# A streaming contrast adjustment: twelve tiles of 32 KB rows become eight tiles of 48 KB rows

## The chip, the cores and the metric

The kernel runs on one core of a Trainium2 chip. The metric is device time in microseconds (us), the median of several runs. A profiled execution gives one more time, together with its span: the time from the first to the last instruction on the core.

The engines that matter are DVE (VectorE), ACT (ScalarE), PE (TensorE), POOL (GpSimd) and the queue of SP (SyncE). Here SP issues all loads and ACT issues all stores. Sixteen DMA engines move the data of both.

## The reference

```python
x: (16, 3, 512, 512) float32, factor = 1.5
mean = np.mean(x, axis=(2, 3), keepdims=True)
return np.clip(mean + factor * (x - mean), 0, 1).astype(np.float32)
```

There are 48 images (16 x 3) of 262,144 pixels. Each image needs its own mean before the first of its pixels can be written. For one image the result is `clip(factor * x + shift, 0, 1)` with `shift = (1 - factor) * mean`. The input and the output have 50.33 MB each.

## The kernel before

The whole input is taken as a flat array. A tile is 128 partitions x 8192 floats: 32 KB in each partition, 4 MB in all. An image then fills 32 partitions, a tile holds four images, and there are twelve tiles. One tensor `ring` in SBUF has six slots of one tile each (192 KB in a partition); tile t uses slot t % 6, and everything is done in place.

For each tile:

- `load` (L82) copies a tile into its slot, issued on SP. At the start six tiles are asked for in four transfers: tiles 0 and 1 alone, then 2 with 3, and 4 with 5. A later load waits until the store that last used its slot has landed.
- `add` (L87 to L100) makes one sum for each partition. ACT copies the slot onto itself and accumulates (L96). PE multiplies these sums by `blockw`, a 128 x 128 matrix that is `(1 - factor) / pixels` inside each 32 x 32 block and zero elsewhere, so that column t of the PSUM tile `bias` holds in every partition the shift of its image (L100). For tile 0 DVE sums the first 4352 columns (L91) beside ACT, and two matmuls are accumulated.
- `clip` (L102 to L114) is two DVE instructions: multiply by the factor and add the shift, which is read from PSUM (L104), then clamp to 0 and 1 (L112).
- `store` (L85) writes the slot back, issued on ACT.

The order on each engine is that of the program text. Tile 0 is clipped and stored in three pieces, of 1024, 2048 and 5120 columns (rows of 4, 8 and 20 KB). Then comes the loop over tiles, L126 to L135: clip of tile t, `add` of tile t+1, store of tile t, load of tile t+5; for t = 1 and 3 the store stands ahead of the `add`. Since the store and the ACT part of `add` are on one queue, a store that stands behind `add(t + 1)` is issued only after tile t+1 has landed and been summed.

Of the kernel before, what the change touches and what calls it, by code (L numbers as in the profile page):

```python
# [1 line left out]

# [4 lines left out]


P = 128  # L10
ROW = 8192
BUFS = 6
FIRST = (1024, 3072)


@with_exitstack
def kernel(
    ctx: ExitStack,
    tc: tile.TileContext,
    x: bass.AP,  # L20
    factor: float,
    out: bass.AP,
):

    nc = tc.nc
    f32 = mybir.dt.float32
    Alu = mybir.AluOpType
    Act = mybir.ActivationFunctionType  # L30

    B, C, H, W = x.shape
    n_img, n_pix = B * C, H * W
    ppi = n_pix // ROW
    per_tile = P // ppi
    n_tiles = n_img // per_tile
    assert ppi * ROW == n_pix and per_tile * n_tiles == n_img

    factor = float(factor)
    wconst = (1.0 - factor) / float(n_pix)  # L40

    x_f = x.rearrange("b c h w -> (b c h w)")
    out_f = out.rearrange("b c h w -> (b c h w)")

    def dram(ap, t, c0=0, c1=ROW, n=1):
        run = [[P * ROW, n]] if n > 1 else []
        return bass.AP(
            tensor=ap.tensor, offset=t * P * ROW + c0, ap=[[ROW, P], *run, [1, c1 - c0]]
        )

    consts = ctx.enter_context(tc.tile_pool(name="consts", bufs=1))
    xpool = ctx.enter_context(tc.tile_pool(name="xpool", bufs=1))
    small = ctx.enter_context(tc.tile_pool(name="small", bufs=1))
    psum = ctx.enter_context(tc.tile_pool(name="psum", bufs=1, space=bass.MemoryType.PSUM))


    sums = small.tile([P, 2 * n_tiles], f32, name="sums")
    bias = psum.tile([P, n_tiles], f32, name="bias")

    blockw = consts.tile([P, P], f32, name="blockw")  # L60
    blocks = blockw.rearrange("p (a b) -> p a b", b=ppi)
    nc.gpsimd.memset(blockw, wconst)  # L62
    for base, step in ((0, -ppi), (ppi - 1, ppi)):
        nc.gpsimd.affine_select(  # L64
            out=blocks,
            in_=blocks,
            compare_op=Alu.is_ge,
            fill=0.0,
            base=base,
            pattern=[[step, per_tile], [0, ppi]],  # L70
            channel_multiplier=1 if step < 0 else -1,
        )


    ring = xpool.tile([P, BUFS, ROW], f32, name="ring")

    def slots(t, n=1, c0=0, c1=ROW):
        k = t % BUFS
        return ring[:, k, c0:c1] if n == 1 else ring[:, k : k + n, :]

    def load(t, n=1):
        nc.sync.dma_start(out=slots(t, n), in_=dram(x_f, t, n=n))  # L82

    def store(t, c0=0, c1=ROW):
        nc.scalar.dma_start(out=dram(out_f, t, c0, c1), in_=slots(t, 1, c0, c1))  # L85

    def add(t, c0=0):  # L87
        own = sums[:, 2 * t : 2 * t + 2]
        parts = []
        if c0:  # L90
            nc.vector.tensor_reduce(  # L91
                out=own[:, 0:1], in_=slots(t, 1, 0, c0), axis=mybir.AxisListType.X, op=Alu.add
            )
            parts.append(own[:, 0:1])
        part = slots(t, 1, c0)
        nc.scalar.activation(out=part, in_=part, func=Act.Copy, accum_out=own[:, 1:2])  # L96
        parts.insert(0, own[:, 1:2])
        shift = bias[:, t : t + 1]
        for k, part in enumerate(parts):
            nc.tensor.matmul(shift, blockw, part, start=k == 0, stop=k == len(parts) - 1)  # L100

    def clip(t, c0=0, c1=ROW):  # L102
        part = slots(t, 1, c0, c1)
        nc.vector.tensor_scalar(  # L104
            out=part,
            in0=part,
            scalar1=factor,
            scalar2=bias[:, t : t + 1],
            op0=Alu.mult,
            op1=Alu.add,  # L110
        )
        nc.vector.tensor_scalar(  # L112
            out=part, in0=part, scalar1=0.0, scalar2=1.0, op0=Alu.max, op1=Alu.min
        )  # L114

    with tc.manual_schedule():
        load(0)
        load(1)
        load(2, 2)
        load(4, 2)  # L120
        add(0, 4352)
        for c0, c1 in zip((0, *FIRST), (*FIRST, ROW)):
            clip(0, c0, c1)
            store(0, c0, c1)
        add(1)
        for t in range(1, n_tiles):  # L126
            clip(t)
            if t in (1, 3):
                store(t)
            if t + 1 < n_tiles:  # L130
                add(t + 1)
            if t not in (1, 3):
                store(t)
            if t + BUFS - 1 < n_tiles:
                load(t + BUFS - 1)  # L135


# [1 line left out]
_INS = ['x', 'factor']  # L139
_OUTS = [((16, 3, 512, 512), 'float32')]  # L140

_NUMBERS = {'factor': 1.5}


# [26 lines left out]
```

## Time and profile before

| what | us |
|---|---|
| median of 3 runs | 239.0 (238.81 to 239.11) |
| profiled execution | 238.72 |
| its span | 237.0 |
| DVE busy | 112.1 |
| ACT busy | 82.9 |
| PE busy | 7.6 |
| mean DMA rate over the span | 425 GB/s |

The profile's page gives the busy time of each engine, then a strip of 40 equal slices of the span in which each digit is the busy share in tenths. Its lines for the queues give the packets, the MB and the share of the sixteen DMA engines' time that these took: q1 carries the loads, q10 the stores. The windows view gives, for any stretch of the span, each engine's busy time, then the granted clock of TensorE (1.00 throughout), the DMA engines' busy share and the GB/s that they moved. Both of these last two count a packet in the window in which it starts, so that short windows are uneven. The waits view says which engine waited for what, for how long in total, how many times, and the longest. In the timeline a group has its start, its length, engine, line, operation, tiles and shapes.

### The profile page before, as it was taken

The numbers are of one execution on the slowest core, as the hardware profiler recorded it, in microseconds if no ns is written. First come the engines' busy times: TensorE is split into PE (matmuls) and PEld (weight loads), VectorE is DVE, ScalarE is ACT, GpSimd is POOL, SyncE is SP. The second block draws the span as 40 slices with busy tenths as digits, with TensorE's granted clock in tenths as the row PEclk, the third lists the DMA queues.
The fourth block names the chain that finished last, engine by engine and source line by source line (L and its number), as shares of the span: only waits on it lengthen the run. The fifth ranks groups of instructions, "written<-read, shape, count | busy, mean of one in ns | idle before, by whom it ended". The sixth has DMA issues, their size and how long they took to land.

```text
span 237.0 us, 211 instructions
## 1 busy us (share of the span) xinstructions
PE 7.6 (3%) x26; PEld 6.5 (3%) x26; DVE 112.1 (47%) x29; ACT 82.9 (35%) x25; POOL 1.0 (0%) x7
## 2 busy tenths in 40 slices
PE   0000000000000000000000000000000000000000
PEld 0000000000000000000000000000000000000000
DVE  0078708609990059979209407704902920950000
ACT  2050190299100894650380091083056029000000
POOL 1000000000000000000000000000000000000000
DMA  7999998999999999999999999999999999999996
GB/s 265 442 442 442 398 459 383 441 428 435 465 426 404 409 442 442 442 442 442 442 426 431 404 420 442 442 442 442 442 442 426 415 398 442 442 442 442 442 442 265
DMA packets 3712, 100.66 MB, mean 425 GB/s; under 512 B 384, under 2 KB 384, under 8 KB 512
## 3 DMA queue, kind: packets, MB, share of 16 engines
q1 hardware_dynamic: 1696, 50.33, 49.6%
q10 hardware_dynamic: 2016, 50.33, 49.2%
HBM read 50.33 MB, written 50.33 MB: 425 GB/s over the span
## 4 chain that ended last, share of the span: by engine, by line
DMA 39%; DVE 25%; another core or an unknown queue 11%; ACT 9%; issue 3%; PE 1%; ACTq 1%; SPq 0%
DMA out_dram<-ring 20%; DMA ring<-in_x_dram 18%; DVE ring L104 11%; DVE ring L112 11%; ACT ring L96 9%; DVE sums L91 2%; PE bias L100 1%; ACTq L85 1%; SPq L82 0%
## 5 line engine op out<-in xcount | busy, mean ns | idle before, releaser
L96 ACT ACTIVATE ring<-ring 128x8192 f32<-128x8192 f32 (+1 forms) x12 | 80.7, 6724 | 117.3 <-DMA ring<-in_x_dram 95.3
L104 DVE TENSOR_SCALAR ring<-ring,bias 128x8192 f32<-128x8192 f32 (+3 forms) x14 | 54.3, 3880 | 84.9 <-PE bias L100 84.9
L112 DVE TENSOR_SCALAR ring<-ring 128x8192 f32<-128x8192 f32 (+3 forms) x14 | 53.4, 3817 | 0.5
L100 PE MATMUL bias<-sums,blockw 128*128 128x1 f32 x26 | 7.6, 361 | 194.0 <-ACT ring L96 193.5
L100 PEld LDWEIGHTS bias<-sums,blockw 128*128 128x128 f32 x26 | 6.5, 312 | 195.0 <-ACT ring L96 177.7
L91 DVE TENSOR_REDUCE sums<-ring 128x1 f32<-128x4352 f32 x1 | 4.7, 4685 | 13.1 <-DMA ring<-in_x_dram 13.1
L96 ACT ACTIVATION_READ_ACCUMULATOR ring<-ring 128x1 f32 x12 | 2.2, 186 | 0.0
L96 ACT ACT_TABLE_LOAD x1 | 1.3, 1283 | 0.8 <-PEq L152 0.8
L64 POOL TENSOR_SCALAR_AFFINE_SELECT blockw<-blockw 128x128 f32<-128x128 f32 x2 | 0.6, 311 | 0.1
L62 POOL MEMSET blockw<- 128x128 f32 x1 | 0.2, 204 | 0.3 <-POOLq L152 0.3
L152 POOL MEMSET const-uint8-127<- 128x1 uint8 x1 | 0.1, 103 | 0.0
L152 POOL MEMSET const-bfloat16-1.0<- 128x1 bf16 x1 | 0.1, 102 | 0.0
L152 POOL MEMSET const-float32-0.0<- 128x1 f32 x1 | 0.1, 98 | 0.3 <-issue 0.3
L152 POOL MEMSET const-float32-1.0<- 128x1 f32 x1 | 0.1, 98 | 0.0
## 6 DMA issues: line engine op xcount, KB each, us to landing
out_dram<-ring ACTq DMA_DIRECT2D x11, 4096.0 KB, 48.5
ring<-in_x_dram SPq DMA_DIRECT2D x8, 4096.0 KB, 31.4
ring<-in_x_dram SPq DMA_DIRECT2D x2, 8192.0 KB, 59.5
out_dram<-ring ACTq DMA_DIRECT2D x1, 2560.0 KB, 37.3
out_dram<-ring ACTq DMA_DIRECT2D x1, 1024.0 KB, 25.8
out_dram<-ring ACTq DMA_DIRECT2D x1, 512.0 KB, 16.1
```

The lines of the kernel that those rows point to most:

```text
L62: nc.gpsimd.memset(blockw, wconst)
L64: nc.gpsimd.affine_select(out=blocks, in_=blocks, compare_op=Alu.is_ge, fill=0.0, base=base, pattern=[[step, per_tile], [0, ppi]], channel ...
L85: nc.scalar.dma_start(out=dram(out_f, t, c0, c1), in_=slots(t, 1, c0, c1))
L91: nc.vector.tensor_reduce(out=own[:, 0:1], in_=slots(t, 1, 0, c0), axis=mybir.AxisListType.X, op=Alu.add)
L96: nc.scalar.activation(out=part, in_=part, func=Act.Copy, accum_out=own[:, 1:2])
L100: nc.tensor.matmul(shift, blockw, part, start=k == 0, stop=k == len(parts) - 1)
L104: nc.vector.tensor_scalar(out=part, in0=part, scalar1=factor, scalar2=bias[:, t : t + 1], op0=Alu.mult, op1=Alu.add,)
L112: nc.vector.tensor_scalar(out=part, in0=part, scalar1=0.0, scalar2=1.0, op0=Alu.max, op1=Alu.min)
L152: nc = _bacc.Bacc("TRN2", target_bir_lowering=False, num_devices=1)
```

## The change

A tile becomes 128 partitions x 12288 floats (48 KB in a partition, 6 MB in all). There are eight tiles and four slots, again 192 KB in a partition. A row of 12288 floats is cut into three thirds of 4096. An image has 64 thirds, which is 21 and a third rows: six images fill a tile, and a partition may hold thirds of two images.

- Sums (`add`): one for each partition and third. DVE reduces the first third, ACT copies and accumulates the other two.
- Shifts (`shifts`, new): `mask` is 1 where a third belongs to an image and 0 elsewhere. DVE multiplies the three sums by the mask (`split`, 128 x 18). Three accumulating matmuls with a constant 128 x 128 matrix `ones` (filled with `(1 - factor) / pixels`) put the six shifts of the tile into every partition (`means`, PSUM). DVE multiplies by the mask again (`spread`) and reduces over the six images, which leaves one shift for each partition and third in SBUF (`shift`).
- `clip`: the multiply is one instruction for each third, since each third has its own shift; the clamp is still one instruction for the piece.
- Transfers: tile 0 is loaded in two parts (rows of 32 and 16 KB) and stored in two (4 and 44 KB). Tiles 1 to 6 are loaded and stored whole, tile 7 is loaded whole and stored in two parts (16 and 32 KB). There are 9 loads and 10 stores, where 10 and 14 stood. Load t+3 is issued once the store of tile t-1 has landed. Each store of tiles 1 to 5 stands behind `add(t + 1)` on ACT.

```diff
-ROW = 8192
-BUFS = 6
-FIRST = (1024, 3072)
+ROW = 12288
+THIRD = 4096
+BUFS = 4
+SPLIT = 8192
+FIRST = 1024
...
+    for base, sign in ((0, 1), (tpi - 1, -1)):
         nc.gpsimd.affine_select(
+            out=mask,
+            in_=mask,
             compare_op=Alu.is_ge,
             fill=0.0,
             base=base,
+            pattern=[[sign, K], [-sign * tpi, per_tile]],
+            channel_multiplier=sign * K,
         )
...
+    def add(t, on_vector=(0,)):
+        for k in range(K):
+            part, own = slot(t, k * THIRD, (k + 1) * THIRD), sums[:, t, k : k + 1]
+            if k in on_vector:
+                nc.vector.tensor_reduce(
+                    out=own, in_=part, axis=mybir.AxisListType.X, op=Alu.add
+                )
+            else:
+                nc.scalar.activation(out=part, in_=part, func=Act.Copy, accum_out=own)
+
+    def shifts(t):
+        full = [P, K, per_tile]
+        nc.vector.tensor_tensor(
+            out=split[:, t], in0=mask, in1=sums[:, t].unsqueeze(2).to_broadcast(full), op=Alu.mult
+        )
+        for k in range(K):
+            nc.tensor.matmul(
+                means[:, t], ones, split[:, t, k], start=k == 0, stop=k == K - 1
             )
+        nc.vector.tensor_tensor(
+            out=spread[:, t], in0=mask, in1=means[:, t].unsqueeze(1).to_broadcast(full), op=Alu.mult
+        )
+        nc.vector.tensor_reduce(
+            out=shift[:, t], in_=spread[:, t], axis=mybir.AxisListType.X, op=Alu.add
+        )
 
     def clip(t, c0=0, c1=ROW):
+        for k in range(c0 // THIRD, (c1 - 1) // THIRD + 1):
+            part = slot(t, max(c0, k * THIRD), min(c1, (k + 1) * THIRD))
+            nc.vector.tensor_scalar(
+                out=part,
+                in0=part,
+                scalar1=factor,
+                scalar2=shift[:, t, k : k + 1],
+                op0=Alu.mult,
+                op1=Alu.add,
+            )
+        part = slot(t, c0, c1)
         nc.vector.tensor_scalar(
             out=part, in0=part, scalar1=0.0, scalar2=1.0, op0=Alu.max, op1=Alu.min
         )
 
     with tc.manual_schedule():
-        load(0)
-        load(1)
-        load(2, 2)
-        load(4, 2)
-        add(0, 4352)
-        for c0, c1 in zip((0, *FIRST), (*FIRST, ROW)):
+        load(0, 0, SPLIT)
+        load(0, SPLIT, ROW)
+        for t in range(1, BUFS):
+            load(t)
+        add(0)
+        shifts(0)
+        for c0, c1 in ((0, FIRST), (FIRST, ROW)):
             clip(0, c0, c1)
             store(0, c0, c1)
+        last = n_tiles - 1
         add(1)
-        for t in range(1, n_tiles):
+        for t in range(1, last):
+            shifts(t)
             clip(t)
-            if t in (1, 3):
-                store(t)
-            if t + 1 < n_tiles:
+            if t + 1 < last:
                 add(t + 1)
-            if t not in (1, 3):
-                store(t)
-            if t + BUFS - 1 < n_tiles:
+            store(t)
+            if t + BUFS - 1 <= last:
                 load(t + BUFS - 1)
+        add(last)
+        shifts(last)
+        for c0, c1 in ((0, THIRD), (THIRD, ROW)):
+            clip(last, c0, c1)
+            store(last, c0, c1)
```

More of the change, by code (lines that the diff above doesn't have):

```diff
@@ L33 @@
     n_img, n_pix = B * C, H * W
-    ppi = n_pix // ROW
-    per_tile = P // ppi
+    K = ROW // THIRD
+    tpi = n_pix // THIRD
+    per_tile = P * K // tpi
     n_tiles = n_img // per_tile
-    assert ppi * ROW == n_pix and per_tile * n_tiles == n_img
+    assert tpi * THIRD == n_pix and per_tile * tpi == P * K
+    assert per_tile * n_tiles == n_img
     factor = float(factor)
@@ L43, with dram @@
     out_f = out.rearrange("b c h w -> (b c h w)")
-    def dram(ap, t, c0=0, c1=ROW, n=1):
-        run = [[P * ROW, n]] if n > 1 else []
+    def dram(ap, t, c0, c1):
         return bass.AP(
-            tensor=ap.tensor, offset=t * P * ROW + c0, ap=[[ROW, P], *run, [1, c1 - c0]]
+            tensor=ap.tensor, offset=t * P * ROW + c0, ap=[[ROW, P], [1, c1 - c0]]
         )
@@ L54 @@
     psum = ctx.enter_context(tc.tile_pool(name="psum", bufs=1, space=bass.MemoryType.PSUM))
[L57 to L63, printed above, removed]
+    sums = small.tile([P, n_tiles, K], f32, name="sums")
+    split = small.tile([P, n_tiles, K, per_tile], f32, name="split")
+    spread = small.tile([P, n_tiles, K, per_tile], f32, name="spread")
+    shift = small.tile([P, n_tiles, K], f32, name="shift")
+    means = psum.tile([P, n_tiles, per_tile], f32, name="means")
+    ones = consts.tile([P, P], f32, name="ones")
+    mask = consts.tile([P, K, per_tile], f32, name="mask")
+    nc.gpsimd.memset(ones, wconst)
+    nc.gpsimd.memset(mask, 1.0)
+    for base, sign in ((0, 1), (tpi - 1, -1)):
         nc.gpsimd.affine_select(
-            out=blocks,
-            in_=blocks,
+            out=mask,
+            in_=mask,
             compare_op=Alu.is_ge,
@@ L69 @@
             base=base,
-            pattern=[[step, per_tile], [0, ppi]],
-            channel_multiplier=1 if step < 0 else -1,
+            pattern=[[sign, K], [-sign * tpi, per_tile]],
+            channel_multiplier=sign * K,
         )
     ring = xpool.tile([P, BUFS, ROW], f32, name="ring")
[L77 to L82, printed above, removed]
@@ L84, in store @@
-    def store(t, c0=0, c1=ROW):
[L85 to L92, printed above, removed]
-            )
[L94 to L100, printed above, removed]
@@ L102, in clip, with slot, load @@
-    def clip(t, c0=0, c1=ROW):
[L103 to L111, printed above, removed]
+    def slot(t, c0=0, c1=ROW):
+        return ring[:, t % BUFS, c0:c1]
+    def load(t, c0=0, c1=ROW):
+        nc.sync.dma_start(out=slot(t, c0, c1), in_=dram(x_f, t, c0, c1))
+    def store(t, c0=0, c1=ROW):
+        nc.scalar.dma_start(out=dram(out_f, t, c0, c1), in_=slot(t, c0, c1))
```

## The prediction

> **What bounds the kernel now.** I read the page first, for who is busy.
>
> ```profile
> PE 7.6 (3%) x26; PEld 6.5 (3%) x26; DVE 112.1 (47%) x29; ACT 82.9 (35%) x25; POOL 1.0 (0%) x7
> ...
> DMA  7999998999999999999999999999999999999996
> ...
> q1 hardware_dynamic: 1696, 50.33, 49.6%
> q10 hardware_dynamic: 2016, 50.33, 49.2%
> ```
>
> No compute engine is busy for half of the span, and the 16 DMA engines are full in every slice but the two ends. The loads (q1) and the stores (q10) together fill 98.8% of the engines' time. Next come the windows, cut where the first packet starts (1.81 us), where transfers land, and where the last packet ends (235.84). The last two columns are the DMA share and GB/s.
>
> ```profile
> 0.00:1.81 1.81, 0.00 (x0) 0.00 (x0) 0.00 (x0) 1.01 (x1) 1.03 (x7) 1.00 0.00 0
> 1.81:12.57 10.76, 0.00 (x0) 0.00 (x0) 0.00 (x0) 0.27 (x1) 0.00 (x0) 1.00 1.06 429
> 12.57:22.25 9.68, 1.15 (x4) 1.00 (x4) 8.39 (x5) 3.50 (x2) 0.00 (x0) 1.00 1.00 433
> 22.25:77.13 54.88, 1.76 (x6) 1.50 (x6) 32.47 (x9) 21.26 (x6) 0.00 (x0) 1.00 1.00 429
> 77.13:193.31 116.18, 4.11 (x14) 3.52 (x14) 62.34 (x14) 49.75 (x14) 0.00 (x0) 1.00 1.00 434
> ...
> 1.81:235.84 234.03, 7.60 (x26) 6.52 (x26) 112.11 (x29) 81.89 (x25) 0.00 (x0) 1.00 1.00 430
> 235.84:237.01 1.17, 0.00 (x0) 0.00 (x0) 0.00 (x0) 0.00 (x0) 0.00 (x0) 1.00 0.00 0
> ```
>
> The reader is to see that the engines never pause between 1.81 and 235.84 us. GB/s is rounded by whole packets, so I take the steady rate from the timeline: the sums that start when a load lands begin at 116.42 and 193.87 us, four rounds apart. Each round moves one load and one store of 4,194,304 bytes in 77.45 / 4 = 19.36 us: 433.25 GB/s. All 100.66 MB at that rate take 232.3 us. The span is then 1.8 (before the first packet) + 232.3 + 1.7 + 1.2 (after the last) = 237.0. The 1.7 is 1.1 in the first transfer (10.76 us, where the next takes 9.68) and about 0.5 in the stage 22 to 77 us: 54.88 x (1 - 429 / 433.25) = 0.54. That is where store pieces of 4, 8 and 20 KB rows run beside loads of 32 KB rows. So whatever shortens no transfer, and starves no queue, is worth nothing here. The waits say the same: the loads wait for slots, that is, for stores.
>
> ```profile
> SPq L82 <- DMA out_dram<-ring: 157.4, 8, 33.3
> ```
>
> And in the timeline's tail the last store is issued long before its turn:
>
> ```profile
> 193.87 7.03 ACT L96 ACTIVATE ring<-ring 128x8192 f32<-128x8192 f32 x1 [12.25 <-DMA ring<-in_x_dram]
> 193.93 0.34 ACTq L85 DMA_DIRECT2D out_dram<-ring  x1
> ...
> 210.65 0.34 ACTq L85 DMA_DIRECT2D out_dram<-ring  x1
> ```
>
> Its 4 MB need 9.68 us before 235.84, so its packets start at about 226.2, some 14.5 us after they could (issue plus the 1.0 us from SP's first issue at 0.80 to the first packet).
>
> **The change part by part.**
>
> *Bytes.* The same 100.66 MB: no change in the 232.3 us but for costs per packet.
>
> *Packets.* One row of a transfer is one packet (12 loads x 128 rows + 10 issues x 16 completion packets = 1696). Each engine moves 96 load rows and 14 x 8 = 112 store rows before, 208. After: loads 8 + 8 + 7 x 8 = 72, stores 8 + 8 + 6 x 8 + 8 + 8 = 80, together 152, so 56 fewer (issues fall from 24 to 19). The price of one packet comes from the DMA view of the stretch in which the first store's 4 KB rows alternate with 32 KB rows.
>
> ```profile
> DMA packets 204, 3.70 MB, mean 404 GB/s; under 512 B 0, under 2 KB 0, under 8 KB 104
> ...
> q1 hardware_dynamic: 100, 3.28, 82.8%
> q10 hardware_dynamic: 104, 0.43, 11.3%
> ```
>
> That window is 24.84 to 34.00 us, 9.16 x 16 = 146.6 engine-us. A 32 KB packet takes 0.828 x 146.6 / 100 = 1213 ns, a 4 KB one 0.113 x 146.6 / 104 = 159 ns. Eight of 159 are 1274, 61 more than one of 1213, so the part that does not scale with bytes is 61 / 7 = 8.7 ns. In the stage 96.49 to 193.31 the two queues' shares add up to 100.4%, so records overlap by 0.4% of 1213, some 5 ns; the true price lies between 4 and 9 ns, and 56 x 4 to 9 = 0.2 to 0.5 us. I take 0.3. A 48 KB row then costs 1.5 x 1213 less 4 ns; no row over 32 KB is in this trace, so this extends the line that 4 and 32 KB make.
>
> *The mixed stage.* The 0.5 us lost there goes with unequal rows. After, there are 4 KB rows beside loads and 44 beside 48 KB, but no 8 or 20 KB pieces. Between 0 and 0.5 us saved; I take 0.1.
>
> *Start and end.* The first load still moves 4 MB in 32 KB rows, so 1.8 + 1.1 stay; the last store has 32 KB rows again, so the 1.2 stays. The new mask on POOL (two memsets, two selects on 18 columns) is done about when the old one was, by 1.8 us, long before the first data at 13.1.
>
> *The sums and shifts: does a queue run dry?* Prices: reduce 4685 / 4352 = 1.077 ns per element, so a third (4096) 4.41 us; ACT 7026 / 8192 = 0.858, so 3.5 + 0.19; multiply 4491 ns per 8192, about 2.35 for a third; clamp 4427 per 8192, about 6.6 for 12288. The three small DVE steps of `shifts` (18 and 3 columns) appear in no row; from nothing up to the 694 ns of a 1024-column clamp each. POOL's 98 to 204 ns rows are nearer in size; I take 0.15. Three matmul pairs at half of the 0.60 that two take: 0.9. So `shifts` is 1.4 us, and DVE needs 4.4 + 1.4 + 7.0 + 6.6 = 19.4 us a tile, ACT 7.4. A tile's load and store need 12.58 MB / 433.25 = 29.0.
>
> Walk: the first 4 MB land at 13.1 as before, the other 2 MB at 17.7; ACT ends the last third at 21.4, shifts 22.8, first store 24.2 (before: 20.0). The rest, 2 x 11264 x 0.55 = 12.4 us, is issued at 36.8 (before: 28.1). The loads cover both: of the 25.2 MB queued up front about 11 MB is left at 36.8. From then both queues share, half each; store 0 ends at 68 and frees slot 0 while tile 3 is still coming. Store t is queued on ACT behind the sums of tile t+1, now for every t (before, stores 1 and 3 went ahead of them), so it waits for load t+1 as well: it is issued at 60.2, 88.6, 117.6, 146.7 for tiles 1 to 4, when the store ahead ends at 68, 97, 126, 155. Some 8 us to spare each round, and a load is under way besides. Load 7 lands at 197.6; sums 7.2, shifts 1.4, a third's multiply and clamp 4.7: issued near 211. The other two thirds, 9.1 more, at 220.1. Store 6 (issued 190.9) and that third keep the engines full until 225.7. The last store could start at 221.1, so 4.6 us are to spare where 14.5 were.
>
> So 24 new small DVE steps, the reduces and the third matmul all hide under transfers; if the tail grew by over 4.6 us, each further us would show.
>
> *Sum:* 237.0 - 0.3 - 0.1 = 236.6 span; the profiled execution was 238.72, so 238.3; the median stands 0.28 above it: **238.6**. About 0.2% (0.48 us) is what a measurement of this kernel can tell from no change, and 0.4 lies inside that.
>
> A rule that speaks against the change: the Trainium skill, "Perfetto Trace Analysis", section DMA Optimizations, says that splitting transfers into smaller chunks can let some start sooner where DMA engines are generally idle. The change does the reverse, but the share of 1.00 says that the engines are not idle, so the rule's condition fails here.
>
> **The rivals.**
>
> *More is saved.* All 9 ns per packet and all of the mixed stage: 0.5 + 0.5 = 1.0 us, 238.0. For it: both ends come from rows. Against it: the overlap of records, and that a 4 KB piece stays. It counts as faster from 0.48 on. Chance 0.29.
>
> *Each transfer has a bare setup.* If 2 us stood free at every issue, five fewer issues would save 10 us: 229. Against it: nine landings between 96 and 193 us without a gap. Chance 0.01. The Trainium skill, "SBUF — State Buffer", section The DMA setup-cost knee, gives about 2 us fixed for each transfer; this trace, with other transfers queued, hides it.
>
> *Long rows run below the line (slower).* 48 KB rows are new, and the mixed stage shows that engines can run at 429. At that rate throughout: 100.66 / 429 = 234.6, 2.3 more: 241. It counts as slower when the steady rate falls under 431.7 (0.9 us more, less the 0.4 saved). Against it: 4 and 32 KB lie on one line. Chance 0.10.
>
> *The last store comes late (slower).* Place: the tail. If multiplies with a shift in SBUF ran at the reduce's 1.08 ns per element instead of 0.55, each tile's would take 13.4 us. Tile 6 would leave DVE at 201.7, the reduce, shifts, and 15.7 + 4.5 of clip would put the last store at 231.0: idle 6.3 us after 225.7, end 244.9. It decides from 4.6 us on. For it: scalars in SBUF are not in the trace. Against it: the clamp, all in SBUF, runs at 0.54. With any other way of a dry queue 0.08; 0.02 for what I did not list.
>
> *The rows are cut again.* If a 48 KB row runs as two packets, packets rise to 264 an engine and 56 x 4 to 9 ns is lost: 239.2 to 239.5. Part of "same", 0.07.
>
> **How the numbers follow.** The forecast with the cut rows holds 0.50 (same); faster 0.29 + 0.01; slower 0.10 + 0.08 + 0.02. The range runs from 238.1, which leaves some 0.08 of the fuller saving out, to 239.6, where a small loss of rate or a dry queue of a us still lies inside and some 0.12 beyond.
>
> **What would show it.** Right: a share of 1.00 from the first to the last packet; about 2,740 packets (152 x 16 + 19 x 16); 12.58 MB every 29.0 us; the last store issued near 220, the transfers' end near 235.4. Wrong: a window below 0.98 before the last store (a dry queue), a steady rate under 432 (long rows), clip rows over 2.6 us for 4096 columns, or a packet count near 4,500 (cut rows).

## The result and the profile after

The changed kernel is slower: 240.75 us median of 6 runs (240.44 to 241.58) against 239.0, a ratio of 1.008 with a 95% interval of 1.0066 to 1.0093. The forecast was 238.6 and its range ended at 239.6. The profiled execution took 240.96 us, with a span of 239.22 (before: 238.72 and 237.01). The runs also lie further apart, 1.1 us from the fastest to the slowest where those of before lie within 0.5.

The page of the changed kernel, busy times, the small new steps and the queues:

```profile
PE 11.6 (5%) x48; PEld 10.8 (5%) x48; DVE 147.3 (62%) x67; ACT 59.9 (25%) x33; POOL 0.9 (0%) x8
...
DMA  7999999998999999999999999999999999999994
...
DMA packets 2737, 100.67 MB, mean 421 GB/s; under 512 B 304, under 2 KB 304, under 8 KB 432
...
q1 hardware_dynamic: 1296, 50.33, 49.5%
q10 hardware_dynamic: 1440, 50.33, 48.7%
q14 instruction: 1, 0.01, 0.0%
...
L110 PE MATMUL means<-split,ones 128*128 128x6 f32 x48 | 11.6, 362 | 195.6 <-DVE split L106 195.6
...
L106 DVE TENSOR_TENSOR split<-mask,sums 128x18 f32<-128x18 f32 x8 | 1.4, 178 | 22.5 <-ACT ring L102 22.4
```

Read from this page alone, nothing is wrong. The packets fell from 3712 to 2737 as counted, both queues together still fill 98.2% of the DMA engines' time, and no compute engine is near its limit. The windows say the same until one looks at two places.

```profile
1.80:12.57 10.77, 0.00 (x0) 0.00 (x0) 0.00 (x0) 0.28 (x1) 0.00 (x0) 1.00 0.99 399
...
42.00:48.00 6.00, 1.45 (x6) 1.35 (x6) 0.99 (x4) 3.89 (x4) 0.00 (x0) 1.00 1.03 373
...
80.00:196.00 116.00, 5.79 (x24) 5.42 (x24) 75.10 (x33) 29.23 (x16) 0.00 (x0) 1.00 1.00 433
...
1.80:237.77 235.97, 11.58 (x48) 10.84 (x48) 147.32 (x67) 58.85 (x33) 0.00 (x0) 1.00 0.99 426
237.77:239.20 1.43, 0.00 (x0) 0.00 (x0) 0.00 (x0) 0.00 (x0) 0.00 (x0) 1.00 0.00 0
```

The main stage runs at 433 GB/s, as before. Between 42 and 48 us, however, the DMA share is 1.03 and only 373 GB/s move: the packets take longer. The same six microseconds of the kernel before:

```profile
42.00:48.00 6.00, 0.00 (x0) 0.00 (x0) 3.32 (x1) 2.27 (x1) 0.00 (x0) 1.00 1.02 437
```

In the trace's packet records every one of the sixteen DMA engines has one 48 KB load row there that takes 2.7 to 3.0 us instead of 1.815. It is the row that stands ahead of the engine's first 44 KB store row.

The second place is the end. Each transfer ends with sixteen completion packets of 4 bytes, one from each DMA engine, so the time between the first and the last of them is how far the engines have drifted apart. First before, in a window from 235.47 to 235.86 us, then the changed kernel, from 235.70 to 237.80. The strips show in 40 slices when something started.

```profile
DMA  0010000000000001000000000000000000000000
...
DMA packets 16, 0.00 MB, mean 0 GB/s; under 512 B 16, under 2 KB 16, under 8 KB 16
```

```profile
DMA  0000000009000000900000000000000000000000
...
DMA packets 18, 0.07 MB, mean 31 GB/s; under 512 B 16, under 2 KB 16, under 8 KB 16
```

Both windows hold the last store's sixteen completions. Before, they lie within 0.35 us (235.48 to 235.83); after, within 2.05 us (235.71 to 237.76), with two late engines still moving whole rows (the two extra packets) when others have ended. The first engine ends only 0.23 us later than before, the mean of the sixteen 0.69 later (236.30 against 235.61). So of the 2.21 us in the span, 0.23 is delay that all engines share, 1.70 is drift between them, and 0.28 is the stretch behind the last packet (1.45 against 1.17).

The tail that the prediction walked is there as forecast, in the timeline:

```profile
212.27 4.61 DVE L123 TENSOR_SCALAR ring<-ring,shift 128x4096 f32<-128x4096 f32 x2
212.39 9.32 ACTq L92 DMA_DIRECT2D out_dram<-ring  x2
216.91 4.43 DVE L132 TENSOR_SCALAR ring<-ring 128x8192 f32<-128x8192 f32 x1
```

The last two stores are issued at 212.4 and 221.4. Store 6 keeps the first engine busy until 221.2, and the first of the two until 226.0: no queue waits for the last tile.

### The profile page after: what moved, and what is told of

Read it like the earlier page. It is cut to its first block, busy times and chain, and to the rows that moved or that the text cites. A ratio compares the mean times of both kernels' runs of the same rounds, so it can differ in the third digit from the quotient of the medians.

```text
span 239.2 us, 286 instructions
## 1 busy us (share of the span) xinstructions
PE 11.6 (5%) x48; PEld 10.8 (5%) x48; DVE 147.3 (62%) x67; ACT 59.9 (25%) x33; POOL 0.9 (0%) x8
## 2 busy tenths in 40 slices
DMA packets 2737, 100.67 MB, mean 421 GB/s; under 512 B 304, under 2 KB 304, under 8 KB 432
## 4 chain that ended last, share of the span: by engine, by line
DMA 40%; another core or an unknown queue 24%; DVE 18%; ACT 8%; PE 2%; SPq 0%; issue 0%; ACTq 0%; DVEq 0%
DMA ring<-in_x_dram 23%; DMA out_dram<-ring 17%; DVE ring L123 9%; DVE ring L132 8%; ACT ring L102 8%; PE means L110 2%; SPq L89 0%; DVE split L106 0%; DVE spread L113 0%; DVE shift L116 0%; ACTq L92 0%; DVEq L106 0%
## 5 line engine op out<-in xcount | busy, mean ns | idle before, releaser
L102 ACT ACTIVATE ring<-ring 128x4096 f32<-128x4096 f32 x16 | 57.7, 3609 | 144.9 <-DMA ring<-in_x_dram 107.4
L98 DVE TENSOR_REDUCE sums<-ring 128x1 f32<-128x4096 f32 x8 | 35.3, 4418 | 38.3 <-DMA ring<-in_x_dram 38.3
L123 DVE TENSOR_SCALAR ring<-ring,shift 128x4096 f32<-128x4096 f32 (+2 forms) x25 | 55.3, 2264 | 0.3
L132 DVE TENSOR_SCALAR ring<-ring 128x12288 f32<-128x12288 f32 (+4 forms) x10 | 52.8, 5280 | 0.3
L110 PE MATMUL means<-split,ones 128*128 128x6 f32 x48 | 11.6, 362 | 195.6 <-DVE split L106 195.6
L110 PEld LDWEIGHTS means<-split,ones 128*128 128x128 f32 x48 | 10.8, 326 | 196.3 <-DVE split L106 196.3
L106 DVE TENSOR_TENSOR split<-mask,sums 128x18 f32<-128x18 f32 x8 | 1.4, 178 | 22.5 <-ACT ring L102 22.4
L113 DVE TENSOR_TENSOR spread<-mask,means 128x18 f32<-128x18 f32 x8 | 1.4, 174 | 12.3 <-PE means L110 12.3
L102 ACT ACTIVATION_READ_ACCUMULATOR ring<-ring 128x1 f32 x16 | 3.0, 186 | 0.0
L116 DVE TENSOR_REDUCE shift<-spread 128x3 f32<-128x18 f32 x8 | 1.4, 172 | 0.3
## 6 DMA issues: line engine op xcount, KB each, us to landing
ring<-in_x_dram SPq DMA_DIRECT2D x7, 6144.0 KB, 36.6
```

What stands on the lines that cost most here:

```text
L98: nc.vector.tensor_reduce(out=own, in_=part, axis=mybir.AxisListType.X, op=Alu.add)
L106: nc.vector.tensor_tensor(out=split[:, t], in0=mask, in1=sums[:, t].unsqueeze(2).to_broadcast(full), op=Alu.mult)
L110: nc.tensor.matmul(means[:, t], ones, split[:, t, k], start=k == 0, stop=k == K - 1)
L113: nc.vector.tensor_tensor(out=spread[:, t], in0=mask, in1=means[:, t].unsqueeze(1).to_broadcast(full), op=Alu.mult)
L116: nc.vector.tensor_reduce(out=shift[:, t], in_=spread[:, t], axis=mybir.AxisListType.X, op=Alu.add)
L123: nc.vector.tensor_scalar(out=part, in0=part, scalar1=factor, scalar2=shift[:, t, k : k + 1], op0=Alu.mult, op1=Alu.add,)
```

## The experiments

Sequences of packets in which each starts where another ended give sixteen chains, one for each DMA engine (the records carry no engine number). "Loss" below is how much longer rows took than the line through 4, 8, 20 and 32 KB rows says (37.66 ns for each KB and 4.4 ns for each row, from start to start), averaged over the engines; "drift" is last less first completion. The first and last completions of the last store, and the drift at the end of the first load, are from each run's profiled execution, one for each run, the medians from its timed runs. The first load of e8 and e12 is the small one of 4 KB rows. The kernel before, timed beside each round, had medians of 238.98 to 239.09.

| run | median us | drift, first load | first / last completion | end drift |
|---|---|---|---|---|
| before | 239.0 | 0.63 | 235.48 / 235.83 | 0.35 |
| after | 240.75 | 1.09 | 235.71 / 237.76 | 2.05 |
| e1, first store whole | 240.94 | 1.06 | 235.65 / 237.22 | 1.57 |
| e2, rows of 32 and 16 KB | 240.83 | 0.94 | 235.93 / 237.68 | 1.75 |
| e3, before, first store whole | 242.26 | 0.80 | 236.17 / 238.67 | 2.50 |
| e4, transfers alone | 239.88 | 1.33 | 235.56 / 236.84 | 1.28 |
| e6, before, 4 and 28 KB | 239.34 | 0.68 | 235.60 / 236.59 | 1.00 |
| e8, small first load | 240.17 | 0.71 | 235.76 / 237.34 | 1.58 |
| e12, before, small first load | 238.99 | 0.55 | 235.62 / 236.10 | 0.47 |
| e16, before, 16 and 16 KB | 238.85 | 0.51 | 235.57 / 235.84 | 0.28 |

In all ten the first engine is done at nearly the same time, within 0.7 us; the times of the last one are spread over 2.8 us. This table is the main finding: what differs between these kernels is mostly how late the last engine is. Of the runs that are not listed, e14, e15 and e17 differ: there the first engine too is late (236.4 to 237.2).

**First round: rows or compute.**

e1, the changed kernel:

```diff
-        for c0, c1 in ((0, FIRST), (FIRST, ROW)):
+        for c0, c1 in ((0, ROW),):
             clip(0, c0, c1)
             store(0, c0, c1)
```

> The changed kernel with tile 0 clipped and stored in one piece of 48 KB rows instead of 4 and 44 KB. Theory A (unequal rows: in the changed kernel's trace all sixteen DMA engines lose about 1.0 us on the load row that stands ahead of the first 44 KB store row, at 44 to 46 us, and the slowest engine's delay sets the end): that loss goes, about 239.8. Theory B (long rows: rows over 32 KB lose time at the borders of transfers, on some engines more than on others): 240.4 to 240.8. Theory C (the new compute steps disturb the transfers): 240.7.

Measured 240.94 (ratio to before 1.0079, 1.0060 to 1.0099), as the change. The loss did not go: it moved to 37 to 46 us, where the first 48 KB store rows now begin, and is 1.2 us. Theory A, that unlike rows are what costs, falls.

e2, the changed kernel:

```diff
+    def cuts(c0, c1):
+        if c0 < SPLIT < c1:
+            return ((c0, SPLIT), (SPLIT, c1))
+        return ((c0, c1),)
     def load(t, c0=0, c1=ROW):
-        nc.sync.dma_start(out=slot(t, c0, c1), in_=dram(x_f, t, c0, c1))
+        for a, b in cuts(c0, c1):
+            nc.sync.dma_start(out=slot(t, a, b), in_=dram(x_f, t, a, b))
...
```

(and `store` alike).

> The changed kernel with every transfer of 48 or 44 KB rows issued as two, cut at column 8192 (rows of 32 and 16 KB, for tile 0's second store 28 and 16 KB); compute, order and slots as they are. Theory B (long rows): the losses at borders go, 238.9 to 239.3, and the runs lie closer together than 240.4 to 241.6. Theory A (unequal rows): alternating 32 and 16 KB rows are more unequal, not less, but the step from 4 to 44 is now from 4 to 28: 240.3 to 241.5. Theory C (compute): 240.7.

Measured 240.83 (1.0064 to 1.0088). No row is longer than 32 KB here and the time is that of the change, so theory B, long rows, falls.

e3, the kernel before:

```diff
-        for c0, c1 in zip((0, *FIRST), (*FIRST, ROW)):
+        for c0, c1 in ((0, ROW),):
             clip(0, c0, c1)
             store(0, c0, c1)
```

> The kernel before with tile 0 clipped and stored in one piece of 32 KB rows instead of 4, 8 and 20 KB. Theory A (unequal rows): the half microsecond that the stage 22 to 77 us loses goes, 238.5. Theories B and C: 239.0, for neither rows nor steps of the main loop change. If instead an early first store matters, later: the first store is issued about 8 us later, so up to 8 us more.

Measured 242.26 (1.0134 to 1.0162): 3.3 us slower, where theory A wanted a gain. It is not that the first store comes too late to be hidden: the DMA share does not fall below 1.00.

```profile
28.00:34.00 6.00, 0.00 (x0) 0.00 (x0) 0.00 (x0) 5.87 (x1) 0.00 (x0) 1.00 1.06 393
34.00:80.00 46.00, 1.76 (x6) 1.50 (x6) 26.66 (x6) 15.38 (x6) 0.00 (x0) 1.00 1.00 433
```

The engines lose 0.9 us on average at 29 to 33 us, when the first 32 KB store rows begin. One row there takes 3.1 us where 1.21 is usual. The engines end 2.5 us apart. The small first pieces of the kernel before, in which I saw a cost of 0.5 us, go with engines that stay together.

e4, the changed kernel:

```diff
     def shifts(t):
-        full = [P, K, per_tile]
-        nc.vector.tensor_tensor(
...
         for k in range(K):
             nc.tensor.matmul(
-                means[:, t], ones, split[:, t, k], start=k == 0, stop=k == K - 1
+                means[:, t, 0:1], ones, sums[:, t, k : k + 1], start=k == 0, stop=k == K - 1
             )
...
     def clip(t, c0=0, c1=ROW):
-        for k in range(c0 // THIRD, (c1 - 1) // THIRD + 1):
...
+            scalar2=means[:, t, 0:1],
```

> The changed kernel's transfers, slots and order, with the compute near that of before: it leaves out the split of sums and shifts by image (each partition's three sums are added into one shift over the whole tile, by three matmuls of one column), and multiplies a whole piece in one DVE instruction, with the shift read from PSUM. Theories A and B (transfers): 240.7, as the changed kernel. Theory C (compute): 238.6 to 239.2.

Measured 239.88 (1.0027 to 1.0051), half way. The loss at the first large store rows is as in the change (1.0 us), and the drift after the first load is even larger (1.33). But from 80 us on the last engine loses nothing more, while the last engine of the change loses 0.85 us there (0.06 at 82.7, 0.38 at 111.8, 0.41 at 170.2, each time on a row at a transfer's border). The instruction packet of q14 is missing here too. So the time depends on more than the list of transfers, against both transfer theories as I had put them. That it is the compute itself is not shown: with less of it e4 also issues its stores at other times (the rest of store 0 at 36.6 us, in the change at 38.2; store 2 at 83.2 and 81.6). And e1, with all the compute of the change, loses only 0.08 us from 90 us on, where e4 loses 0.07 and the change 0.24. The next round did not settle it.

**Second round: the first stores and the first load.** From e3 I formed theory D.

e5 and e7 (e7 with e4's compute):

```diff
-FIRST = 1024
+FIRST = (1024, 3072, 7168)
...
-        for c0, c1 in ((0, FIRST), (FIRST, ROW)):
+        for c0, c1 in zip((0, *FIRST), (*FIRST, ROW)):
```

> The changed kernel with tile 0 stored in pieces of 4, 8, 16 and 20 KB rows instead of 4 and 44. Theory D (the first full-size store rows, begun while the loads run alone and the sixteen DMA engines are in step, cost each engine about 1 us and unevenly; small, growing first stores spread this out, as the three pieces of the kernel before do): the loss of about 0.95 us at 44 us falls to 0.3 to 0.5, 239.9 to 240.2. Theory A (unequal rows cost, each kind anew): slower than the changed kernel, 241 or more. Theory E (the engines are spread already by their first load rows, which have a pitch of 48 KB, and the last one sets the end): little change, 240.4 to 240.7.

> The changed kernel's transfers with the compute near that of before (one shift for the whole tile, the split by image left out, as in the run of the transfers alone), and tile 0 stored in pieces of 4, 8, 16 and 20 KB rows. Theory D alone: 239.88 less 0.5 to 0.7, so 239.2 to 239.4. If the compute and its longer program are the other part, this one stays about 0.9 below the changed kernel with the same pieces.

Measured 241.02 (240.47 to 243.01) and 240.75 (240.28 to 241.68), neither better than with 4 and 44 KB (240.75 and 239.88). The loss where the large store rows begin did fall, as theory D says: at 36 to 60 us it is 0.36 in e5 and 0.47 in e7, where the change has 0.98. But the time did not follow. Store 0, now in four pieces, landed at 75.8 to 77.0, load 4 was issued only at 77.4 and 77.1, and load 3 had ended on the first engine at 66.0 and 66.2: for eleven microseconds no load was queued. In e5 the drift then grew from 1.22 us (at 76) to 3.41, in e7 from 0.78 to 1.77. And the 0.9 us by which less compute was faster is down to 0.3 within runs that lie 2.5 us apart, so this pair neither confirms nor refutes it.

e6, the kernel before:

```diff
-FIRST = (1024, 3072)
+FIRST = (1024,)
```

> The kernel before with tile 0 stored in pieces of 4 and 28 KB rows instead of 4, 8 and 20. Theory D: the step from 4 to 28 KB costs most of what a single 32 KB first store cost (242.26 against 239.0), 240.0 to 241.5. If only an early first store matters (it is issued at 20 us here as before): 239.0.

Measured 239.34 (1.0001 to 1.0019): some 0.3 us, less than theory D wanted, with 0.6 us of loss at the first stores and 1.0 of drift. It is also a little over the 239.0 that an early first store alone would give.

e8, the changed kernel:

```diff
-        load(0, 0, SPLIT)
+        load(0, 0, FIRST)
+        load(0, FIRST, SPLIT)
```

> The changed kernel with a load of 4 KB rows ahead of the first load, which then has 28 KB rows. Theory E (spread set by the first load rows): small first rows start the engines closer together, and the end comes 0.5 to 0.9 us earlier, 239.9 to 240.3. Theory D and the compute theory: 240.7.

Measured 240.17 (1.0030 to 1.0054), 0.6 us better than the change and as theory E expected. The engines are 0.71 us apart after the first small load and 0.64 after the first tile, instead of 1.09. This edit changes nothing but the first rows of the changed kernel, and it shows that there a smaller spread at the start reaches the end. That is no rule for all runs: e4 starts with the widest spread of the table (1.33) and ends with 1.28, and e10 below starts closer together without a gain.

**Third round: the pitch in HBM, and whether engines share work.**

e9, the kernel before, with tiles 0 to 7 as the first 32 KB of 48 KB rows:

```diff
+        if t < 8:
+            run = [[P * WIDE, n]] if n > 1 else []
+            return bass.AP(
+                tensor=ap.tensor, offset=t * P * WIDE + c0, ap=[[WIDE, P], *run, [1, c1 - c0]]
+            )
...
```

> The kernel before, moving the same arrays in rows of 32 KB that start 48 KB apart in HBM: tiles 0 to 7 are the first 32 KB of each 48 KB row, tiles 8 to 11 the remaining 16 KB pieces, two to a partition. It leaves out the right grouping of rows into images. Theory E1 (the pitch of 48 KB spreads the engines): the spread of the engines at the end of the first load grows from 0.63 us to about 1.0, and the end is at 239.6 to 240.6. Theory E2 (the spread comes from the larger tiles and fewer slots, or from the first store rows): 239.0 to 239.3.

Measured 249.47 (1.0368 to 1.0451), which no theory had. Up to 115 us it goes like before, with a drift of 0.93 after the first load and 0.62 later. Then come the tiles made of 16 KB pieces: their loads alternate packet by packet with stores of 32 KB rows and get a third of the bytes, so loads come late, and from 190 us on the DMA share is 0.84 (358 GB/s). The total says nothing of the pitch.

e10, the run e2 with its rows next to each other:

```diff
+        if c0 < SPLIT:
+            width, first, col = SPLIT, t * P * SPLIT, c0
+        else:
+            width = ROW - SPLIT
+            first, col = n_tiles * P * SPLIT + t * P * width, c0 - SPLIT
         return bass.AP(
-            tensor=ap.tensor, offset=t * P * ROW + c0, ap=[[ROW, P], [1, c1 - c0]]
+            tensor=ap.tensor, offset=first + col, ap=[[width, P], [1, c1 - c0]]
         )
```

> The changed kernel with every transfer in rows of 32 and 16 KB, as in the run with rows of 32 and 16 KB (240.83), but with these rows next to each other in HBM (pitch 32 KB and 16 KB) instead of 48 KB apart; slots, order and compute unchanged. It leaves out the right grouping of rows into images. Theory E1 (pitch): 239.2 to 239.8. Theory E2 (tile size, slots, first store rows) and the compute theory: 240.6 to 241.0.

Measured 240.73, as e2. The drift after the first load fell from 0.94 to 0.66 and that at the end from 1.75 to 1.25, but the first engine is done 0.14 us later, and the time did not follow. Over all runs that start with rows of 32 KB, the drift after the first load is 0.80 to 1.37 us with a pitch of 48 KB (ten runs) and 0.51 to 0.80 with 32 KB (six). So the pitch shows in the start, and e10 says that it is not what decides the whole.

e11, the kernel before with one more load:

```diff
+        nc.sync.dma_start(
+            out=extra[0:51, :],
+            in_=bass.AP(tensor=x_f.tensor, offset=0, ap=[[ROW, 51], [1, 512]]),
+        )
         add(0, 4352)
```

> The kernel before with one more load, of 51 partitions with 2 KB each (0.1 MB, 0.1% of the bytes), which should run on three of the sixteen DMA engines, 17 rows each (51 = 3 x 17), about 17 x 80 ns = 1.4 us of each. Theory E (every engine has a fixed share of each transfer, none takes over another's work, and the last one sets the end): 1.1 to 1.4 us slower, 240.1 to 240.5. If the engines share the work: 0.24 us at the most, 239.1 to 239.3.

Measured 252.39 (1.0473 to 1.0554): 13 us for 0.1% more bytes. The page and the windows of e11:

```profile
DMA  7999999999999999999999999999999999869086
```

```profile
216.00:226.00 10.00, 0.00 (x0) 0.00 (x0) 1.22 (x1) 6.16 (x1) 0.00 (x0) 1.00 0.68 292
226.00:236.00 10.00, 0.58 (x2) 0.50 (x2) 8.33 (x2) 0.96 (x2) 0.00 (x0) 1.00 0.41 177
```

The 51 small rows fall on three engines, 17 on each. They run from 78 to 101 us, one at a time between 32 KB store rows, so for 17 turns the loads of these engines move 2 KB a turn. Their later rows land 6.8 us after those of the first engine. A tile is there only when all sixteen have landed; the first engine goes on in rounds of 19.36 us and has loaded its share of tile 11 by 193 us. After that it has only stores left, which wait for tiles that the three engines still have to load, and the share falls to 0.68 and 0.41. No engine takes over another's rows. The size I had expected missed the turns.

e12, the kernel before:

```diff
-        load(0)
+        load_part(0, 0, 1024)
+        load_part(0, 1024, ROW)
         load(1)
```

(`load_part` loads some columns of a tile.)

> The kernel before with a load of 4 KB rows ahead of the rest of tile 0. Theory E: in the changed kernel this brought 240.17 against 240.75; here the spread at the end is only 0.35 us, so at most 0.3 is to be had: 238.7 to 239.0. If the small load costs anything by itself: above 239.1.

Measured 238.99 (ratio 1.000, 0.9991 to 1.0008): nothing to gain here, at the edge of what was expected.

**Fourth round: the length of the first store rows.** Open was which part makes the loss at the first stores. e13 and e14 set `FIRST` in the changed kernel to 6144 and 4096, e15 adds a small first load to e14, e16 sets it to `(4096,)` in the kernel before:

```diff
-FIRST = 1024
+FIRST = 6144
```

> The changed kernel with tile 0 stored in two pieces of 24 and 24 KB rows instead of 4 and 44: the same number of transfers. Theory S (when store rows begin or grow longer beside full loads, every DMA engine loses time once, about 0.025 us for each KB of the largest rise: 0.4 us for the rise of 12 KB in the kernel before, 0.9 for 32, 1.0 for 40, 1.2 for 48): the rise is 24, the loss 0.6 instead of 1.0, and the end 0.3 to 0.6 earlier, 240.1 to 240.4. Theory L (the loss is one of the start of large stores, whatever the rise): 240.6 to 240.9.

> The changed kernel with tile 0 stored in two pieces of 16 and 32 KB rows. Theory S: each rise is 16 KB, the loss about 0.45, the end 0.5 to 0.8 earlier, 239.9 to 240.2. Theory L: 240.6 to 240.9.

> The changed kernel with a load of 4 KB rows ahead of the first load, and tile 0 stored in pieces of 16 and 32 KB rows. Theories S and E together: the run with the small load alone (240.17) less 0.5 to 0.8, so 239.4 to 239.7, with the engines less than 1 us apart at the end. If both only shift the same loss: 240.1.

> The kernel before with tile 0 stored in two pieces of 16 KB rows instead of 4, 8 and 20 KB. Theory S: rises of 16 and 16 instead of 4, 4, 12 and 12: 239.0 to 239.3, as near to before as the pieces of 4 and 28 KB (239.34) or nearer. Theory L: 240 or more.

Measured 242.14, 242.92, 241.91 and 238.85. Theory S expected gains in the first three, and they came out 1.2 to 2.2 us above the change. The loss at the first stores is about 0.7 to 0.9 us, lower than 1.0 but not as theory S sized it, and a new loss of 0.9 to 1.8 us appears at 76 to 90 us. In e13's chain of waits one can see what goes before it, and in its windows the price:

```profile
38.22 38.82 DMA out_dram<-ring
77.03 0.02 issue
77.05 0.03 SPq L89
77.08 0.03 issue
77.11 35.52 DMA ring<-in_x_dram
```

```profile
79.00:89.00 10.00, 1.45 (x6) 1.35 (x6) 8.29 (x6) 4.46 (x4) 0.00 (x0) 1.00 0.99 388
89.00:196.00 107.00, 4.34 (x18) 4.06 (x18) 67.75 (x28) 21.92 (x12) 0.00 (x0) 1.00 1.00 432
```

Load 4 waits for store 0 until 77.1 us, but the first engine was through with load 3 at 74.7. The load queue was empty, and when it began anew beside full store rows the engines lost time once more. An empty queue alone is not shown to be the cause: in e7 it was empty for longer (66.2 to 77.1 us), its load rows began anew at 81.3, and its engines lost 0.18 us between 60 and 80 us and nothing between 80 and 90. In the kernel before the next load is issued at 65.6, 11 us before the queue would be empty (76.9); in the changed kernel at 74.1, 5.7 us before (79.8).

e16 is as good as before (ratio 0.9992, 0.9983 to 1.0000) and has the smallest drift of the table. Its last store's completions, in a window from 235.55 to 235.87:

```profile
DMA  0000000000000000010001100000100000000000
...
DMA packets 16, 0.00 MB, mean 0 GB/s; under 512 B 16, under 2 KB 16, under 8 KB 16
```

**Last round.** e17 sets `FIRST` to 3072 in the changed kernel, and e18 adds the small first load.

> The changed kernel with tile 0 stored in pieces of 12 and 36 KB rows instead of 4 and 44; store 0 should still land before load 3 has ended, so that the load queue does not run empty (it did at 76 us in the runs with 24 and 24, and 16 and 32 KB). Theory R (the engines lose time, unevenly, whenever one queue starts anew from empty beside the other's long rows, and each rise of the first store rows is part of that): the loss at the first stores falls from 1.0 to about 0.6 to 0.8, nothing is lost at 80 to 88 us, 240.2 to 240.6. Theory L (a fixed cost): 240.7 to 241. If the loss near 80 us in those runs had nothing to do with the empty load queue: 241.5 or more.

> The same with a load of 4 KB rows ahead of the first load. Theory R with theory E: the gain of the small first load (0.6) comes on top, 239.6 to 240.0; the engines end about 1 us apart. If the two do not add up: 240.1 to 240.3.

Measured 242.48 for e17 (1.0123 to 1.0157). The loss at the first stores was about 0.9, but store 0's engines were 3.0 us apart, load 4 was issued at 78.1, after the first engine had ended load 3 at 76.4, and 1.2 us were lost at 80 to 90. The condition of the test, a load queue that stays filled, was not met. e18's executions lie between 239.65 and 244.98, so it settles nothing.

No version was measured that beats the kernel before by more than its interval.

## Why the prediction was wrong, point by point

- *Bytes and packets*: right. 2737 packets, as counted, and a main stage no slower: the first engine completes a store every 29.00 us (72.53, 101.53, 130.54, 159.54, 188.54), 12.58 MB / 29.00 = 433.9 GB/s where before had 433.25. The rival of long rows falls with this and with e2.
- *The walk of sums, shifts and stores*: right where it mattered, that no queue runs dry, with two errors that stayed hidden. Stores 1 to 4 were forecast at 60.2, 88.6, 117.6 and 146.7 and came at 61.6, 81.6, 110.7 and 139.9; the last at 221.4 for 220.1. Stores 2 to 4 are some 7 us early, for a store that stands behind sums on ACT is issued when the tile has landed, and not only when it has been summed, as I had said of both kernels: the sums of tile 4 start at 110.62, and store 3 is issued at 110.73 (before: the sums of tile 11 at 193.87, store 10 at 193.93). And store 0 was to end at 68, where half of 433 GB/s from 36.8 us on would give about 64; it ended at 72.5 to 73.7. Its 44 KB rows, issued at 38.2, began at 46.6 to 47.7, for its eight 4 KB rows on each engine took eight turns with 48 KB load rows. Shifts were dearer, 178 ns instead of 150 for a small DVE step and 1.45 us instead of 0.9 for the matmuls, all hidden. The rival of a late last store falls: multiplies of 4096 columns took 2.35 us with the shift in SBUF.
- *The step that failed*: "The 1.7 is 1.1 in the first transfer and about 0.5 in the stage 22 to 77 us", of which I kept the first part and let the second shrink by 0.1. The first part kept its size on average (0.74 us of loss up to 13 us, before 0.68) but spread wider (1.09 for 0.63). The second, which was to be 0.4, doubled: from 0.48 before to 1.0, nearly all of it in the one step from 4 to 44 KB rows. In all, losses averaged over the engines are about 2.0 us where before has 1.1, 0.24 of them after 90 us, where before has none.
- *The assumption beneath it*: I treated sixteen engines as one. The page's share cannot tell an engine that is late from one that is slow everywhere. So none of the signs that the prediction names for being wrong appeared: no window below 0.98 before the last store, no rate under 432 in the steady stage, no clip row over 2.6 us, no cut rows. Nor is any of its rivals what happened; for what it did not list it left a chance of 0.02. The engine that ends last lost 1.56 us at its first row, 1.20 at 44 us and 0.85 at three later borders, 3.6 in all. The last one of before lost 0.6 to 1.0 at its first row and 0.6 in the mixed stage, 1.2 to 1.6. The difference of 2.0 to 2.4, less 0.3 for the packets saved, is 1.7 to 2.1; the last completions are 1.93 apart.
- *The mixed stage read the wrong way round*: its 0.5 us was counted as a cost of small pieces that a change might save. e3 shows that without them the kernel before is 3.3 us slower.

What is shown: part of the slowdown comes from the first load rows (0.6 us back in e8), and part goes with less compute at equal transfers or with the other issue times that come with it (0.9 us in e4, not confirmed by the pair e5 and e7). The loss when large store rows begin is in every trace of the change and of its versions; every version that lowered it by other first store pieces also emptied the load queue, and none of them was faster. Why engines lose time there, why those already late lose more at later borders, and what in e4 takes part, stays open.

## What to carry to other kernels

When the DMA share is 1.00, look at the spread of the completion packets of each transfer: the engines have fixed shares, and the last one's delay is the kernel's. In the changed kernel 2.8 of the 3.6 us that the last engine lost were lost in the first 50 us, where the first rows of each direction begin, so a new tile size needs that stage measured anew. A stretch that looks like a small cost (mixed rows at 429 GB/s) should be taken out in a run before it is booked as a saving.

## What was not expected of the hardware

- Turns between the two queues go by packet, whatever its length, and one row of up to 48 KB is one packet. In e11 51 rows of 2 KB held up the loads of three engines by 17 turns and cost 13 us.
- With 286 instead of 211 instructions in the profile, an 8 KB instruction packet (q14) runs at 179.8 us, while the stores and loads go on. On the engine that carries it the packet takes 0.31 us, and the load row behind it 0.53 us more than others. In the change that engine was not the last; in e1 it ended within 0.01 us of the last.
- A drift once made can stay for the rest of the run: in the kernel before it is 0.35 us in every transfer from 77 us to the end, in e6 0.98 to 1.00 in every store from 53 us on. In the change it grew, from 1.14 us in the store that ended at 72.5 to 2.05 in the one at 188.5. In e4 the stores' drift fell from 2.45 to 1.28 once the loads had ended (at 196 to 199 us).
